# One-hot tiles of a gate matrix: tokens interleaved in pairs instead of in fours

## The chip, the cores and the metric

The kernel runs on one core of a Trainium2 chip. The metric is the device time of one execution in microseconds. Before the change it is 3146.83 us, the median of three runs (3141.98 to 3147.86).

## The reference

The reference is a decoder trunk of two layers over 512 tokens of width 1024. In each layer a mixer (differential attention, a short convolution and gated linear attention) is followed by PEER, a mixture of 16384 experts of one neuron each. Only PEER matters here. Each of its 8 heads scores 128 keys twice, takes the 16 best of each half, combines them and keeps the 16 best pairs; a pair names the expert `e1 * 128 + e2`, and a softmax over the 16 scores is its gate:

```python
e1 = jnp.take_along_axis(i1, ci // PEER_TOPK, axis=-1)
e2 = jnp.take_along_axis(i2, ci % PEER_TOPK, axis=-1)
experts = (e1 * PEER_NKEYS + e2).reshape(T, hk)
gates = jax.nn.softmax(sc, axis=-1).reshape(T, hk)
...
hb = jax.nn.gelu(jnp.einsum('tkd,td->tk', ub, xb), approximate=False)
return jnp.einsum('tk,tkd->td', gb * hb, vb)
```

So each token has 128 chosen experts (8 heads of 16), with rows `ub` and `vb` taken from two tables of 16384 rows.

## The kernel before

Of the 512 tokens, the last 128 are done by gathering rows (`gathered`, L719): GpSimd fetches one row per token at a time (L715), and VectorE multiplies and sums it (L723, L732). The first 384 tokens are done densely: for each chunk `c` of 128 experts, TensorE computes the hidden values of all 384 tokens (`hidden`, L639, tile `psh`, 24 matmuls of 384 columns), ScalarE applies the gelu (L645), and later, in a second sweep, the hidden values are multiplied by a gate (L813) and by the table `v` (`accumulate`, L824, tiles `pv`, matmuls of 512 columns). The gate is zero for every expert that a token didn't choose. f32 values are split into a high and a low part (`split`, L629: a cast on ScalarE at L630 and a subtraction on VectorE at L631), and each product takes three matmuls (`mm3`, L73 to L77).

The gates of all 384 tokens and 16384 experts are the gate matrix `G` in DRAM. It is built while the first sweep runs. `route` (L878) finds, for 128 tokens, the expert numbers and gates, and leaves them transposed as f16 tiles with 128 chosen experts in the partitions and the tokens along the free dimension: `E1` and `E2` (the two halves of the expert's number) and `GH` and `GL` (the gate, high and low). `gate_matrix` (L952) then takes 16 tokens at a time, which is one one-hot tile. VectorE writes four tiles of 128 partitions by 2048 f16:

- `A` (L964) is 1 where the row number equals the token's `E1`, `B` (L965) where it equals its `E2`; the row number comes from the constant `iota4`.
- `AH` (L966) and `AL` (L967) are `A` times the gate's high and low part.

For each token, TensorE then multiplies `B` by `AH` and by `AL` into one 128 by 128 block of `psg` (L972, L973), which is the token's gates for all experts. Four tokens fill one PSUM tile of 512 columns, which ScalarE evacuates (L975), and a DMA on ScalarE's queue writes the 16 tokens to `G` (L976). In the profile the tiles are called `oha` (A), `ohb` (B), `ohh` (AH) and `ohl` (AL). PSUM pool `psA`, from which `psg` comes, has four buffers, `B`, `AH` and `AL` have two each, `A` has one.

The tokens lie interleaved in these tiles: in the free dimension the order is group of four tokens, then row number 0 to 127, then the token in the group. So the VectorE operations read and write runs of four f16, and the 128 columns that TensorE reads for one token, as weights and as columns that it streams, are four f16 apart.

The order of the work is set by the program: the loop at L762 goes over the 72 chunks of the first sweep and 3 more, and after each chunk's `hidden` it draws from a generator as much routing and one-hot work as costs 2.72 us by an estimate written in the code (4.6 for one one-hot tile), and some steps of `gathered`. There are 24 one-hot tiles per layer, in three bursts of eight, and routing between them; 48 tiles in all, each with 32 pairs of weight load and matmul.

Of the kernel before, what the change touches and what calls it, by code (L numbers as in the profile page):

```python
# [10 lines left out]
F16 = mybir.dt.float16  # L11
# [8 lines left out]
P = 128  # L20
# [26 lines left out]
OHT = 16  # L47
# [12 lines left out]
def bc(ap, pattern):  # L60
    return bass.AP(tensor=ap.tensor, offset=ap.offset, ap=[ap.ap[0]] + pattern)


class K:
# [35 lines left out]
    def constants(self, scratch):  # L100
        nc, cp = self.nc, self.cp
        self.identb = cp.tile([P, P], BF16, name="identb")
        nc.scalar.copy(self.identb, self.ident)
        self.one = cp.tile([P, 1], F32, name="one")
        nc.vector.memset(self.one, 1.0)
        self.causal = cp.tile([P, P], BF16, name="causal")
        nc.gpsimd.memset(self.causal, 0.0)
        nc.gpsimd.affine_select(out=self.causal, in_=self.causal, compare_op=OP.is_ge, fill=-1.0e30,
                                base=0, pattern=[[-1, P]], channel_multiplier=1)
        self.starts = cp.tile([P, 16], F16, name="starts")  # L110
        self.dstart = cp.tile([P, 16], F16, name="dstart")
        self.iota16 = cp.tile([P, 16], F16, name="iota16")
        for j in range(16):
            nc.vector.memset(self.starts[:, j:j + 1], float(GRP_START[j]))
            nc.vector.memset(self.dstart[:, j:j + 1], float(GRP_START[j] - (GRP_START[j - 1] if j else 0)))
            nc.vector.memset(self.iota16[:, j:j + 1], float(j))
        self.iota4 = cp.tile([P, P, 4], F16, name="iota4")
        nc.gpsimd.iota(self.iota4, pattern=[[1, P], [0, 4]], base=0, channel_multiplier=0,
                       allow_small_or_imprecise_dtypes=True)
        used = 0  # L120

        def temp(*shape):
            nonlocal used
            n = math.prod(shape)
            t = scratch[:, used:used + n]
            used += n
            return t.rearrange("p (a b) -> p a b", b=shape[1]) if len(shape) > 1 else t

        pos_i = temp(TB).bitcast(I32)
        nc.sync.dma_start(pos_i, self.ins["positions"].rearrange("(b p) -> p b", p=P))  # L130
        pos = temp(TB)
        nc.vector.tensor_copy(pos, pos_i)
        ang = temp(TB, 8)
        for j in range(8):
            nc.vector.tensor_scalar(ang[:, :, j], pos, INV_FREQ[j], None, op0=OP.mult)
        res = []
        for name, shift in (("cos", 0.25), ("sin", 0.0)):
            n = temp(TB, 8)
            nc.vector.tensor_scalar(n, ang, 1.0 / (2 * math.pi), shift, op0=OP.mult, op1=OP.add)
            nc.vector.tensor_scalar(n, n, MAGIC, None, op0=OP.add)  # L140
            nc.vector.tensor_scalar(n, n, MAGIC, None, op0=OP.subtract)
            r = temp(TB, 8)
            prev = ang
            for c in TWO_PI:
                nc.vector.scalar_tensor_tensor(r, n, -c, prev, op0=OP.mult, op1=OP.add)
                prev = r
            if shift:
                nc.vector.tensor_scalar(r, r, math.pi / 2, None, op0=OP.add)
            nc.vector.tensor_scalar(r, r, 3.1415925, -3.1415925, op0=OP.min, op1=OP.max)
            t = cp.tile([P, TB, 8], F32, name=name)  # L150
            nc.scalar.activation(t, r, AF.Sin)
            res.append(t)
        self.cos, self.sin = res
# [43 lines left out]
        lo = self.act.tile([P, KD, T], F32R, tag="alo", name="alo")  # L197
        return hi, lo

    # ---------------------------------------------------------------- mixer  # L200
    def mixer(self, L):
        nc, tc, ins = self.nc, self.tc, self.ins
        lam_init = 0.8 - 0.6 * math.exp(-0.3 * L)
# [399 lines left out]
            self.head_out(of, ggain, mgh[:, :, t0:t0 + P], mgl[:, :, t0:t0 + P])  # L603
            yield 4

    # ---------------------------------------------------------------- peer
    def peer(self, L, xh, xl, rest):
        nc, tc, ins = self.nc, self.tc, self.ins
        G = self.dr.tile([NCH // GE, P, TD // TBAT, GE * TBAT], F32, tag="G", name="G")
# [342 lines left out]
    def gate_matrix(self, bt, E1, E2, GH, GL, G, hp):  # L952
        nc = self.nc
        stg = hp.tile([P, NCH, TBAT], F32, tag="stg", name="stg")
        for o in range(TBAT // OHT):
            t0 = bt * TBAT + o * OHT
            ng = OHT // 4
            tok = lambda t: bc(t[:, t0:t0 + OHT], [[4, ng], [0, P], [1, 4]])
            io = bc(self.iota4, [[0, ng], [4, P], [1, 4]])
            B = hp.tile([P, ng, P, 4], F16, tag="ohb", name="ohb")  # L960
            A = hp.tile([P, ng, P, 4], F16, tag="oha", name="oha", bufs=1)
            AH = hp.tile([P, ng, P, 4], F16, tag="ohh", name="ohh")
            AL = hp.tile([P, ng, P, 4], F16, tag="ohl", name="ohl")
            nc.vector.tensor_tensor(A, io, tok(E1), op=OP.is_equal)  # L964
            nc.vector.tensor_tensor(B, io, tok(E2), op=OP.is_equal)  # L965
            nc.vector.tensor_tensor(AH, A, tok(GH), op=OP.mult)  # L966
            nc.vector.tensor_tensor(AL, A, tok(GL), op=OP.mult)  # L967
            yield 4.6
            for g in range(ng):
                ps = self.psA.tile([P, 4, P], F32, tag="a", name="psg")  # L970
                for j in range(4):
                    nc.tensor.matmul(ps[:, j], B[:, g, :, j], AH[:, g, :, j], start=True, stop=False)  # L972
                    nc.tensor.matmul(ps[:, j], B[:, g, :, j], AL[:, g, :, j], start=False, stop=True)  # L973
                q = o * OHT + g * 4
                nc.scalar.activation(stg[:, :, q:q + 4].rearrange("p e t -> p t e"), ps, AF.Copy, scale=1.0 / GSCALE)  # L975
        nc.scalar.dma_start(G[:, :, bt].rearrange("g p w -> p g w"), stg.rearrange("p (g e) t -> p g (e t)", e=GE))  # L976
# [70 lines left out]
```

## Time and profile before

| | |
|---|---|
| Runs, median of three | 3146.83 us |
| Profiled execution, first to last instruction (its span) | 3145.6 us |
| Mean granted TensorE clock | 0.995 |
| One-hot matmuls (L972, L973), number | 768 + 768 |
| One-hot matmuls, mean duration of one | 297 and 298 ns |
| VectorE's four one-hot operations, number and mean of one | 4 × 48, 1.22 us |
| Evacuations of `psg` on ScalarE, number and mean of one | 192, 1.108 us |

The profiled execution has no time of its own beside its span; the span is 1.2 us under the median of the runs and inside their range, so sums against it are compared with the median. PE is TensorE's matmuls and PEld its weight loads, which overlap with them; DVE is VectorE, ACT ScalarE, POOL GpSimd. Matmuls are pipelined, so durations of neighbours overlap and what one costs is read from the distance of starts.

### The profile page before, as it was taken

The numbers are of one execution on the slowest core, as the hardware profiler recorded it, in microseconds if no ns is written. First come the engines' busy times: TensorE is split into PE (matmuls) and PEld (weight loads), VectorE is DVE, ScalarE is ACT, GpSimd is POOL, SyncE is SP. The second block draws the span as 40 slices with busy tenths as digits, with TensorE's granted clock in tenths as the row PEclk, the third lists the DMA queues.
The fourth block names the chain that finished last, engine by engine and source line by source line (L and its number), as shares of the span: only waits on it lengthen the run. The fifth ranks groups of instructions, "written<-read, shape, count | busy, mean of one in ns | idle before, by whom it ended". The sixth has DMA issues, their size and how long they took to land.

```text
span 3145.6 us, 45595 instructions
## 1 busy us (share of the span) xinstructions
PE 3083.6 (98%) x16742; PEld 2742.6 (87%) x16742; DVE 2473.3 (79%) x5079; ACT 1269.1 (40%) x1874; POOL 731.4 (23%) x543
## 2 busy tenths in 40 slices
PE   8999999999999999999999999999999999999998
PEld 7777889999999999788878788999999999987886
DVE  5776999968678787877766769998677878878777
ACT  5243345455333333333352533455553333323333
POOL 0000000211355554322200000002113555453221
PEclk9999999999999999999999999999999999999999
DMA  4112247788998888999722212478899988989996
GB/s 120 54 54 80 94 135 233 251 286 271 320 345 326 326 317 303 361 335 333 283 75 68 68 66 94 156 227 269 269 293 339 329 326 322 324 313 351 329 344 237
DMA packets 335665, 757.03 MB, mean 241 GB/s; under 512 B 30001, under 2 KB 192209, under 8 KB 331345
## 3 DMA queue, kind: packets, MB, share of 16 engines
q1 hardware_dynamic: 141904, 407.00, 36.5%
q0 software_dynamic: 73728, 268.47, 24.2%
q10 hardware_dynamic: 119808, 78.66, 8.0%
q8 instruction: 131, 2.15, 0.3%
q14 instruction: 94, 0.76, 0.1%
HBM read 673.28 MB, written 80.74 MB: 240 GB/s over the span
## 4 chain that ended last, share of the span: by engine, by line
PE 79%; DVE 6%; issue 6%; DMA 4%; POOL 3%; ACT 2%; SPq 0%; POOLq 0%; ACTq 0%; DVEq 0%
PE psh L77 9%; PE psh L75 9%; PE psh L76 9%; PE pv L77 9%; PE pv L76 9%; PE pv L75 9%; POOL row L715 3%; DMA row<-in_v_rows,idx 3%; PE psg L972 3%; PE psg L973 3%; PE psp L77 2%; PE psp L76 2%; PE psp L75 2%; PE psq L76 2%; PE psq L77 2%
## 5 line engine op out<-in xcount | busy, mean ns | idle before, releaser
L715 POOL DMA_INDIRECT row<-in_u_rows,idx x256 | 375.1, 1465 | 1407.5 <-DVE si L873 689.5
L75 PE MATMUL psh<-ahi,uh 128*128 128x384 f32 x2048 | 693.1, 338 | 2.0 <-ACT ht L645 2.0
L77 PE MATMUL psh<-ahi,ul 128*128 128x384 f32 x2048 | 688.4, 336 | 6.5 <-DVE ul L631 6.5
L76 PE MATMUL psh<-alo,uh 128*128 128x384 f32 x2048 | 687.3, 336 | 0.0
L75 PE MATMUL pv<-vh,wh 128*128 128x512 f32 x1536 | 597.6, 390 | 7.7 <-ACT wh L815 7.7
L77 PE MATMUL pv<-vh,wl 128*128 128x512 f32 x1536 | 601.3, 392 | 0.0
L76 PE MATMUL pv<-vl,wh 128*128 128x512 f32 x1536 | 600.6, 391 | 0.0
L715 POOL DMA_INDIRECT row<-in_v_rows,idx x256 | 339.1, 1324 | 595.2 <-DVE yacc L732 547.4
L631 DVE TENSOR_TENSOR ul<-uraw,uh 128x1024 fp32r<-128x1024 f32 x288 | 350.9, 1221 | 138.5 <-ACT uh L630 127.2
L630 ACT CAST uh<-uraw 128x1024 fp32r<-128x1024 f32 x288 | 302.5, 1052 | 315.4 <-PE psh L76 217.1
L645 ACT ACTIVATE ht<-psh 128x384 f32<-128x384 f32 x256 | 125.2, 489 | 709.0 <-PE psh L77 708.9
L75 PEld LDWEIGHTS psh<-ahi,uh 128*128 128x128 f32 x2048 | 387.4, 189 | 7.0 <-ACT ht L645 2.6
L77 PEld LDWEIGHTS psh<-ahi,ul 128*128 128x128 f32 x2048 | 386.3, 189 | 7.2 <-DVE ul L631 7.2
L76 PEld LDWEIGHTS psh<-alo,uh 128*128 128x128 f32 x2048 | 386.7, 189 | 4.1
L801 DVE TENSOR_TENSOR vl<-vraw,vh 128x1024 fp32r<-128x1024 f32 x256 | 312.7, 1221 | 79.4 <-issue 63.2
L75 PEld LDWEIGHTS pv<-vh,wh 128*128 128x128 f32 x1536 | 288.7, 188 | 67.1 <-ACT wh L815 10.0
L77 PEld LDWEIGHTS pv<-vh,wl 128*128 128x128 f32 x1536 | 289.2, 188 | 62.3 <-DVE wl L801 1.9
L76 PEld LDWEIGHTS pv<-vl,wh 128*128 128x128 f32 x1536 | 289.0, 188 | 59.5 <-DVE vl L801 1.0
L732 DVE SCALAR_TENSOR_TENSOR yacc<-row,wk,yacc 128x1024 f32<-128x1024 f32 x254 | 325.8, 1283 | 10.3 <-DMA row<-in_v_rows,idx 8.7
L723 DVE SCALAR_TENSOR_TENSOR gscr<-row,xg 128x1024 f32<-128x1024 f32 x256 | 312.5, 1221 | 13.9 <-DMA row<-in_u_rows,idx 12.0
L815 ACT CAST wh<-ht 128x384 fp32r<-128x384 f32 x256 | 130.8, 511 | 386.7 <-PE pv L76 218.9
L806 ACT CAST vh<-vraw 128x1024 fp32r<-128x1024 f32 x256 | 268.4, 1049 | 23.3 <-DMA vraw<-in_v_rows 22.1
(285 smaller groups left out, 4663.0 us busy)
## 6 DMA issues: line engine op xcount, KB each, us to landing
uraw<-in_peer_u SPq DMA_DIRECT2D x256, 512.0 KB, 4.8
vraw<-in_v_rows SPq DMA_DIRECT2D x256, 512.0 KB, 6.3
G<-stg ACTq DMA_DIRECT2D x48, 1024.0 KB, 6.5
g<-G SPq DMA_DIRECT2D x32, 1536.0 KB, 10.1
H<-ht ACTq DMA_DIRECT2D x144, 192.0 KB, 4.4
ht<-H SPq DMA_DIRECT2D x144, 192.0 KB, 5.7
wraw<-in_w_in SPq DMA_DIRECT2D x96, 256.0 KB, 2.9
uraw<-in_peer_w_q SPq DMA_DIRECT2D x32, 512.0 KB, 3.6
```

Of the source, the lines that this page charges most:

```text
L75: mm(ps, ah, bh, start=first, stop=False)
L76: mm(ps, ah, bl, start=False, stop=False)
L77: mm(ps, al, bh, start=False, stop=last)
L630: pin(nc.scalar.copy(hi, src))
L631: self.last = pin(nc.vector.tensor_tensor(lo, src, hi.bitcast(F32), op=OP.subtract))
L645: pin(nc.scalar.activation(hs[c], ps, AF.Gelu))
L715: nc.gpsimd.indirect_dma_start(out=r, out_offset=None, in_=ins[name], in_offset=bass.IndirectOffsetOnAxis(ap=idx[:, k:k + 1], axis=0))
L723: nc.vector.scalar_tensor_tensor(sc, r, 1.0, xg, op0=OP.mult, op1=OP.mult, accum_out=hd[:, k:k + 1])
L732: nc.vector.scalar_tensor_tensor(yacc, r, wk[:, k:k + 1], yacc, op0=OP.mult, op1=OP.add)
L801: self.last = pin(nc.vector.tensor_tensor(lo, src, hi.bitcast(F32), op=OP.subtract))
L806: pin(nc.scalar.copy(vh[c], vs[c]))
L815: pin(nc.scalar.copy(wh[c], hs[c]))
```

## The change

The tokens are interleaved in pairs: the order in the free dimension is pair of tokens, row number, token in the pair. The constant that holds the row numbers has two copies of each number instead of four. The VectorE operations have the same number of elements; their token operand now consists of runs of two f16, each read 128 times before the next. The four tokens of one PSUM tile now come from two pairs, and the 128 columns of a token are two f16 apart. The number and the order of the instructions on all engines, the buffers and the DMAs are the same.

```diff
-        self.iota4 = cp.tile([P, P, 4], F16, name="iota4")
-        nc.gpsimd.iota(self.iota4, pattern=[[1, P], [0, 4]], base=0, channel_multiplier=0,
+        self.iota2 = cp.tile([P, P, 2], F16, name="iota2")
+        nc.gpsimd.iota(self.iota2, pattern=[[1, P], [0, 2]], base=0, channel_multiplier=0,
...
-            ng = OHT // 4
-            tok = lambda t: bc(t[:, t0:t0 + OHT], [[4, ng], [0, P], [1, 4]])
-            io = bc(self.iota4, [[0, ng], [4, P], [1, 4]])
-            B = hp.tile([P, ng, P, 4], F16, tag="ohb", name="ohb")
-            A = hp.tile([P, ng, P, 4], F16, tag="oha", name="oha", bufs=1)
-            AH = hp.tile([P, ng, P, 4], F16, tag="ohh", name="ohh")
-            AL = hp.tile([P, ng, P, 4], F16, tag="ohl", name="ohl")
+            ng = OHT // 2
+            tok = lambda t: bc(t[:, t0:t0 + OHT], [[2, ng], [0, P], [1, 2]])
+            io = bc(self.iota2, [[0, ng], [2, P], [1, 2]])
+            B = hp.tile([P, ng, P, 2], F16, tag="ohb", name="ohb")
+            A = hp.tile([P, ng, P, 2], F16, tag="oha", name="oha", bufs=1)
+            AH = hp.tile([P, ng, P, 2], F16, tag="ohh", name="ohh")
+            AL = hp.tile([P, ng, P, 2], F16, tag="ohl", name="ohl")
...
-            for g in range(ng):
+            for g in range(OHT // 4):
                 ps = self.psA.tile([P, 4, P], F32, tag="a", name="psg")
                 for j in range(4):
-                    nc.tensor.matmul(ps[:, j], B[:, g, :, j], AH[:, g, :, j], start=True, stop=False)
-                    nc.tensor.matmul(ps[:, j], B[:, g, :, j], AL[:, g, :, j], start=False, stop=True)
+                    at = (slice(None), g * 2 + j // 2, slice(None), j % 2)
+                    nc.tensor.matmul(ps[:, j], B[at], AH[at], start=True, stop=False)
+                    nc.tensor.matmul(ps[:, j], B[at], AL[at], start=False, stop=True)
```

## The prediction

> **What bounds the kernel now.** I read the page first: its engine totals and the chain that ended last.
>
> ```profile
> span 3145.6 us, 45595 instructions
> PE 3083.6 (98%) x16742; PEld 2742.6 (87%) x16742; DVE 2473.3 (79%) x5079; ACT 1269.1 (40%) x1874; POOL 731.4 (23%) x543
> PE 79%; DVE 6%; issue 6%; DMA 4%; POOL 3%; ACT 2%; SPq 0%; POOLq 0%; ACTq 0%; DVEq 0%
> ```
>
> TensorE carries 79% of the chain. The next question is whether it is also the bound where the changed code runs. The second layer's gate stage is cut here into its three bursts of eight one-hot tiles (first, third and fifth row) and the routing between them. Columns: window, its length, busy time of PE, PEld, DVE, ACT and POOL, granted clock, DMA share, GB/s.
>
> ```profile
> 2013.00:2093.00 80.00, 80.00 (x541) 78.30 (x541) 71.89 (x175) 49.31 (x59) 3.78 (x4) 1.00 0.69 211
> 2093.00:2160.00 67.00, 67.00 (x392) 66.95 (x391) 61.73 (x162) 30.41 (x42) 9.44 (x8) 1.00 0.77 261
> 2160.00:2241.00 81.00, 81.00 (x551) 79.29 (x549) 67.35 (x75) 47.29 (x57) 15.50 (x11) 1.00 0.87 277
> 2241.00:2274.00 33.00, 33.00 (x194) 32.97 (x193) 17.57 (x20) 12.11 (x19) 4.68 (x5) 1.00 0.83 275
> 2274.00:2355.00 81.00, 81.00 (x550) 79.29 (x550) 61.86 (x66) 47.26 (x57) 14.80 (x12) 1.00 0.87 274
> sum 342.00, PE 342.00 PEld 336.79 DVE 280.40 ACT 186.37 POOL 48.20; mean PE 68.40 PEld 67.36 DVE 56.08 ACT 37.27 POOL 9.64
> ```
>
> TensorE never idles in these 342 us at full granted clock, so time taken off its stream comes off the kernel, until VectorE (133.6 of the first 147 us) or the DMA engines (0.87) stand in the way. A busy PE is not a PE at its peak, so the timeline of TensorE comes next, at the start of a burst: start, duration, instruction.
>
> ```profile
> 452.72 0.33 PE L76 MATMUL psh<-alo,uh 128*128 128x384 f32 x1
> ...
> 453.41 0.34 PE L77 MATMUL psh<-ahi,ul 128*128 128x384 f32 x1
> 453.59 0.29 PE L972 MATMUL psg<-ohh,ohb 128*128 128x128 f16 x1
> 453.69 0.30 PE L973 MATMUL psg<-ohl,ohb 128*128 128x128 f16 x1
> 453.81 0.30 PE L972 MATMUL psg<-ohh,ohb 128*128 128x128 f16 x1
> 453.93 0.30 PE L973 MATMUL psg<-ohl,ohb 128*128 128x128 f16 x1
> ...
> 456.42 0.30 PE L972 MATMUL psg<-ohh,ohb 128*128 128x128 f16 x1
> ```
>
> ```profile
> 1299.81 0.39 PE L75 MATMUL pv<-vh,wh 128*128 128x512 f32 x1
> ...
> 1301.40 0.39 PE L76 MATMUL pv<-vl,wh 128*128 128x512 f32 x1
> ```
>
> Durations overlap, so starts are what to read. The 384-column matmuls start 0.1725 us apart (452.72 to 453.41, four steps), the 512-column ones 0.227 us apart (seven steps): 128 more columns cost 0.0545 us, and 0.009 us is left for each load and matmul pair. The one-hot matmuls have only 128 columns, and should on that scale start 0.0635 us apart. They start 0.1187 us apart (453.69 to 456.42, 23 steps). Taking 0.009 off, a column costs 0.86 ns where the others pay 0.43: a factor of two. What differs is the operand: before the change the columns of one token lie four f16, 8 bytes, apart; the fast matmuls read 4-byte columns that touch.
>
> **The change part by part.** No instruction is added, removed or moved; only the iota constant halves (outside the loops, once). What changes is the address pattern of three reads: TensorE's columns (8 bytes apart, now 4), its weights likewise, and the token operand of four VectorE operations (runs of four, now two).
>
> TensorE's columns. Four-byte spacing is what the f32 rows above read at 0.43 ns a column, so I take 0.0635 us for a pair. The lower bound is the only 16-bit matmul with touching columns, whose successor starts 0.06 us later:
>
> ```profile
> 191.60 0.22 PE L439 MATMUL pss<-causal,identb 128*128 128x128 bf16 x1
> 191.66 0.33 PE L438 MATMUL pss<-kT,qz 128*128 128x128 f32 x1
> ```
>
> The upper bound is no gain, 0.1187. By the middle one, each pair saves 0.0552 us; 48 tiles of 32 pairs make 1536 pairs, so 84.8 us for the kernel, 42.4 per layer, 1.77 per tile. With 0.06 it would be 90 us. [...]
>
> TensorE's weights. These are the groups by form; columns: count | busy us, mean ns | idle before.
>
> ```profile
> L973 PEld LDWEIGHTS <-ohb 128*128 128x128 f16 x768 | 90.2, 117 | 1.4
> L439 PEld LDWEIGHTS <-identb 128*128 128x128 bf16 x64 | 6.3, 99 | 4.7 <-issue 2.4
> L75 PEld LDWEIGHTS psh<-ahi,uh 128*128 128x128 f32 x2048 | 387.4, 189 | 7.0 <-ACT ht L645 2.6
> ```
>
> A load lasts 117 ns against 99 with touching columns; it should come down between. It runs beside the previous matmul, so I cost it at nothing. Its cover gets thinner, though: in the one-hot stream each load starts with a matmul and the next matmul starts when it ends. If that end were a hard condition, the cover is gone at 99 ns; the f32 loads speak against it, since they last 189 ns in a stream that starts every 173. That is the third rival.
>
> VectorE. Four operations a tile, 192 in all:
>
> ```profile
> L965 DVE TENSOR_TENSOR ohb<-iota,E 128x2048 f16<-128x2048 f16 x48 | 58.7, 1222 | 29.9 <-PE psg L973 29.9
> L966 DVE TENSOR_TENSOR ohh<-oha,GH 128x2048 f16<-128x2048 f16 x48 | 58.6, 1220 | 4.1 <-PE psg L972 4.1
> L923 DVE TENSOR_TENSOR ge<-ci,starts 128x2048 f16<-128x2048 f16 x8 | 18.3, 2282 | 0.0
> L920 DVE TENSOR_TENSOR pr<-pr 128x2048 f16<-128x2048 f16 x8 | 9.8, 1219 | 0.1
> L920 DVE TENSOR_TENSOR pr<-pr 128x1024 f16<-128x1024 f16 x16 | 11.2, 699 | 0.1
> L920 DVE TENSOR_TENSOR pr<-pr 128x256 f16<-128x256 f16 x8 | 3.5, 442 | 0.1
> L469 DVE TENSOR_TENSOR ho<-po,ry 128x512 f32<-128x512 f32 x8 | 5.5, 692 | 0.4
> ```
>
> They take 1.22 us for 2048 elements, two a cycle; L923, whose token operand repeats single elements, takes 2.28, one a cycle. Runs of two are not in the trace as a repeated operand. Bounds: 1.22 (as now) and 2.28 (single elements); a gain is excluded, because the unbroken 2048-element row (L920) is no shorter. The nearest row for runs of two is L920's last pass, 256 elements in 442 ns. From 2048 and 1024 elements (1219, 699) an element costs 0.508 ns, so 256 would take 309 at two a cycle and 439 at one. It runs at one. But there every run of two is followed by a jump of 32 bytes in all three operands, while in the change the output and the iota are unbroken and the token operand reads one 4-byte word again and again, which L469 does with an f32 word at full pace: 512 elements at one a cycle in 692 ns, as many cycles as 1024 packed ones in 699. I take 1.22 us, as nearer to the last, and keep 2.28 as the rival. [...]
>
> What is late next. In the first burst and the routing behind it (2013 to 2160), TensorE's 147 us would shrink by eight tiles' 14.2 to 132.8, below VectorE's own 133.6. VectorE's look-ahead is two one-hot buffers and three weight chunks, so some waits stay, an estimated 4 us: about 138 us, and 5 of 14.2 us are not collected. In the other 195 us TensorE would need 166.7; VectorE 146.8, ScalarE 106.7. The DMA engines were busy for 0.87×81 + 0.83×33 + 0.87×81 = 168 us there, so they would be full. What they moved in each fortieth of the span:
>
> ```profile
> GB/s 120 54 54 80 94 135 233 251 286 271 320 345 326 326 317 303 361 335 333 283 75 68 68 66 94 156 227 269 269 293 339 329 326 322 324 313 351 329 344 237
> ```
>
> They are not yet at their most: 276 GB/s would become 323, and later slices hold up to 361. I charge 3 us.
>
> ScalarE's four evacuations per tile are not hidden within a burst:
>
> ```profile
> L975 ACT ACTIVATE stg<-psg 128x512 f32<-128x512 f32 x192 | 185.0, 1108 | 7.0 <-PE psg L973 7.0
> L630 ACT CAST uh<-uraw 128x1024 fp32r<-128x1024 f32 x288 | 302.5, 1052 | 315.4 <-PE psh L76 217.1
> L645 ACT ACTIVATE ht<-psh 128x384 f32<-128x384 f32 x256 | 125.2, 489 | 709.0 <-PE psh L77 708.9
> ```
>
> 4 × 1.108 = 4.43 us against 32 × 0.0635 = 2.03 on TensorE. But four PSUM buffers take a whole tile, and the next tile comes at least 24 × 0.1725 = 4.14 us later; a cycle of one tile and one chunk needs 5.97 us of ScalarE against 6.17 of TensorE. So nothing is charged, with the tightest margin of all.
>
> Sum: 42.4 − 5 − 3 = 34.4 per layer, about 69 us in both. The profiled span is 3145.6 us, 1.2 below the median of 3146.83 and inside the runs' 3141.98 to 3147.86. So 3146.8 − 69 = 3078 us.
>
> **The rivals.** *VectorE falls to one element a cycle.* Each of 192 operations costs 1.06 us more, 4.25 per tile. VectorE then needs 133.6 + 34 = 167.6 us where there are 147, 118.9 where there are 114, and 61.9 + seven tiles' 29.8 = 91.7 where there are 81: 36 us more per layer, and some 6 of waits. That is 84 us more, 3231, whatever TensorE gains. In the first stretch it takes over from (147 − 133.6 − 4)/32 = 0.3 us more per operation; with about 0.55 more the stage as a whole is slower than today (137.6 + 150.8 + 96 × 0.56 = 342). For: the L920 row. Against: no jumps here.
>
> *TensorE's reading is not what is slow.* Then the factor of two has another cause, such as any spacing other than touching, and two f16 apart is as slow as four. Time: 3147. For: no row shows 16-bit columns with gaps smaller than four. Against: the f32 rows read the same byte spacing at full pace. [...]
>
> *The weight load binds.* If a matmul must wait for the whole load, a pair takes 0.100 us (99 ns and the start), so 0.0187 × 1536 = 29 us gross; VectorE and the DMA engines cover that nearly whole: 3120 us.
>
> **How the numbers follow.** Forecast 0.60, VectorE slow 0.19, no change 0.15, load-bound 0.06. The likeliest case gives 3078; its own range is 3052 (0.06 a pair, nothing lost: 90, and a few us of run-to-run spread) to 3100 (9 us of the first stretch and, if the DMA engines hold up the later bursts, half of their 28.3: 23 per layer). The load-bound and unchanged cases lie up to 3153; together these hold about 0.8, so the range is 3052 to 3153 and leaves out the slow VectorE. A measurement of this kernel can tell about 0.2%, 6 us, from no change. Faster: 0.60 + 0.06 = 0.66; same 0.15; slower 0.19.
>
> **What would show it.** Right: one-hot matmuls starting about 0.064 us apart; the four VectorE groups still at 1.22 us; a burst of a tile 2.0 instead of 3.8 us; TensorE's first idle time in the gate stage, before psh, released by VectorE's ul. Wrong: VectorE groups at 2.28 us with TensorE waiting for ohh or ul; starts still 0.119 apart; starts at 0.100 with each load ending at a matmul's start; or a DMA share near 1.0 with VectorE waiting for row.

## The result, and the profile after

The changed kernel takes 3074.93 us (median of four runs, 3068.26 to 3076.22), the kernel before 3145.01 us beside it (3141.98 to 3147.86). The ratio is 0.9774, 95% interval 0.9763 to 0.9786: 70 us faster. The forecast was 3078 us. The time of every kernel is the median of its fast executions; of the kernel with columns in pairs one execution of four was slow, at 4738.76 us, and isn't counted.

First the page of the changed kernel: the span, the busy time of each engine, and the chain that ended last.

```profile
span 3066.5 us, 45595 instructions
PE 2996.6 (98%) x16742; PEld 2657.9 (87%) x16742; DVE 2470.3 (81%) x5079; ACT 1268.5 (41%) x1874; POOL 739.7 (24%) x543
PE 74%; issue 7%; DVE 7%; POOL 4%; DMA 3%; ACT 3%; ACTq 1%; SPq 0%; POOLq 0%; DVEq 0%
```

PE has 87 us less busy time, PEld 85 less, and no other engine has changed by more than 9. TensorE's part of the chain fell from 79% to 74%, and ScalarE's DMA issues (ACTq) have come in with 1%. The profiled execution took 3068.26 us (its span is 1.8 us less), 6.7 us under the median of the runs, so the account of the whole gain at the end of this text uses a later profile of the same kernel, whose time is the median.

Now the one-hot burst itself. This is TensorE's timeline in the changed kernel, from the last matmul before a tile to the first one behind it: start, duration, instruction.

```profile
459.60 0.34 PE L77 MATMUL psh<-ahi,ul 128*128 128x384 f32 x1
459.78 0.23 PE L973 MATMUL psg<-ohh,ohb 128*128 128x128 f16 x1
459.85 0.22 PE L974 MATMUL psg<-ohl,ohb 128*128 128x128 f16 x1
...
461.57 0.22 PE L974 MATMUL psg<-ohl,ohb 128*128 128x128 f16 x1
461.60 0.42 PE L75 MATMUL psh<-ahi,uh 128*128 128x384 f32 x1
```

The tile lasts 1.82 us (459.78 to 461.60), and from 459.85 to 461.57 are 30 steps of 0.0573 us. Before, a step was 0.1187 us and a tile took 3.70 us. The groups by form show the same, and also what did not change (count | busy us, mean ns | idle before):

```profile
L973 PE MATMUL psg<-ohh,ohb 128*128 128x128 f16 x768 | 93.9, 219 | 0.4 <-ACT stg L976 0.4
L974 PEld LDWEIGHTS <-ohb 128*128 128x128 f16 x768 | 74.5, 97 | 0.7 <-issue 0.7
L964 DVE TENSOR_TENSOR oha<-iota,E 128x2048 f16<-128x2048 f16 x48 | 58.5, 1218 | 0.1
L966 DVE TENSOR_TENSOR ohh<-oha,GH 128x2048 f16<-128x2048 f16 x48 | 58.5, 1218 | 0.0
L976 ACT ACTIVATE stg<-psg 128x512 f32<-128x512 f32 x192 | 186.0, 1121 | 12.2 <-issue 9.9 <-PE psg L974 2.3
```

A matmul's record is 78 ns shorter (219 against 297), a load's 20 ns (97 against 117). VectorE's operations take 1.22 us as before. The four evacuations of a tile still take 4.5 us beside a burst of 1.82 us, and TensorE waited 0.4 us for them in the whole run.

For the stage as a whole, here is the second layer cut at the ends of the bursts: the first burst with the routing behind it, the second with its routing, and the third. The first fence is before, the second after. Columns: window, its length, busy time of PE, PEld, DVE, ACT and POOL, granted clock, DMA share, GB/s.

```profile
2013.50:2160.80 147.30, 147.30 (x933) 145.53 (x933) 133.92 (x337) 79.74 (x101) 13.22 (x11) 1.00 0.73 234
2160.80:2274.70 113.90, 113.90 (x741) 112.16 (x741) 84.82 (x95) 59.37 (x75) 20.37 (x17) 1.00 0.86 275
2274.70:2354.90 80.20, 80.20 (x545) 78.65 (x545) 61.16 (x64) 47.16 (x57) 14.58 (x11) 1.00 0.88 276
```

```profile
1972.20:2108.70 136.50, 134.12 (x932) 132.53 (x931) 133.15 (x337) 79.54 (x100) 13.28 (x11) 0.99 0.78 252
2108.70:2208.20 99.50, 99.23 (x742) 97.78 (x740) 84.39 (x95) 59.25 (x75) 23.38 (x17) 1.00 0.93 315
2208.20:2273.50 65.30, 65.30 (x546) 64.20 (x545) 57.47 (x60) 44.33 (x53) 16.71 (x10) 1.00 0.95 312
```

By the median of the 48 tiles, a tile takes 1.888 us less (3.705 before, 1.817 after), and eight of them make 15.1 us for each stretch. The second and third collect 14.4 and 14.9 of it, and in them TensorE is still busy throughout, at a DMA share of 0.93 and 0.95. The first collects 10.8, and there VectorE is busy for 133.15 of 136.5 us (2.2 us of its idle time wait for ScalarE's cast, 1.1 for TensorE) while TensorE idles 2.4. The first layer reads 10.2, 14.6 and 14.9. So the gate stages give 79.8 us together.

Not all of that arrives. From the end of the first layer's last burst to the second layer's first one-hot matmul it took 1218.5 us before and 1221.0 after, and from the second layer's last burst to the end 790.7 and 793.0: 4.8 us are given back. The rest of the difference between the two spans, 4.1 us, lies before the first one-hot matmul (453.6 against 449.5 us), where the change does nothing; that start differs from run to run, and in the repetition below it is at 452.8.

### The profile page after: what moved, and what is told of

Same layout as the page of the kernel before. It is cut to its first block, busy times and chain, and to the rows that moved or that the text cites. A ratio compares the mean times of both kernels' runs of the same rounds, so it can differ in the third digit from the quotient of the medians.

```text
span 3066.5 us, 45595 instructions
## 1 busy us (share of the span) xinstructions
PE 2996.6 (98%) x16742; PEld 2657.9 (87%) x16742; DVE 2470.3 (81%) x5079; ACT 1268.5 (41%) x1874; POOL 739.7 (24%) x543
## 4 chain that ended last, share of the span: by engine, by line
PE 74%; issue 7%; DVE 7%; POOL 4%; DMA 3%; ACT 3%; ACTq 1%; SPq 0%; POOLq 0%; DVEq 0%
PE pv L77 9%; PE pv L75 9%; PE pv L76 9%; PE psh L75 8%; PE psh L77 8%; PE psh L76 8%; POOL row L715 4%; PE psp L77 2%; PE psp L76 2%; PE psp L75 2%; DMA row<-in_v_rows,idx 2%; PE psq L76 2%; PE psq L77 2%; PE psq L75 2%; PE pst L545 1%
## 5 line engine op out<-in xcount | busy, mean ns | idle before, releaser
L715 POOL DMA_INDIRECT row<-in_u_rows,idx x256 | 390.6, 1526 | 1315.9 <-DVE si L873 669.5
L715 POOL DMA_INDIRECT row<-in_v_rows,idx x256 | 331.5, 1295 | 601.5 <-DVE yacc L732 565.7
L645 ACT ACTIVATE ht<-psh 128x384 f32<-128x384 f32 x256 | 125.3, 489 | 612.4 <-PE psh L77 605.5
```

The lines of the kernel that those rows point to most:

```text
L645: pin(nc.scalar.activation(hs[c], ps, AF.Gelu))
L715: nc.gpsimd.indirect_dma_start(out=r, out_offset=None, in_=ins[name], in_offset=bass.IndirectOffsetOnAxis(ap=idx[:, k:k + 1], axis=0))
```

## Where the rest of the gain went: two waits to explain

Before the change TensorE waits for nothing in the gate stages. In the changed kernel one long wait comes in each first stretch, and others follow at the end of the stages. The waits are given here from one start to the next; the idle time that the profile prints in brackets is some 0.3 us less. The long one is 3.2 us in the first layer and 2.7 in the second. TensorE's timeline in the first:

```profile
527.22 0.34 PE L77 MATMUL psh<-ahi,ul 128*128 128x384 f32 x1
530.40 0.45 PE L75 MATMUL psh<-ahi,uh 128*128 128x384 f32 x1 [2.85 <-ACT ht L645]
...
531.16 0.52 PE L75 MATMUL psh<-ahi,uh 128*128 128x384 f32 x1
531.48 0.52 PE L76 MATMUL psh<-alo,uh 128*128 128x384 f32 x1
```

Behind the wait, matmuls of 384 columns start 0.32 us apart for about ten matmuls, where they start every 0.173 us otherwise. TensorE waited for ScalarE's gelu (L645), because no buffer of `psh` was free. ScalarE's timeline says why the gelu was late; ACTq is a DMA issue.

```profile
518.31 0.38 ACTq L977 DMA_DIRECT2D G<-stg  x1
...
519.79 7.12 ACTq L769 DMA_DIRECT2D H<-ht  x1
526.94 1.28 ACT L898 ACT_TABLE_LOAD   x1 [6.24 <-issue]
528.23 0.31 ACT L898 ACTIVATE gt<-gt 128x128 f32<-128x128 f32 x1
528.56 1.28 ACT L645 ACT_TABLE_LOAD   x1
529.86 0.49 ACT L645 ACTIVATE ht<-psh 128x384 f32<-128x384 f32 x1
```

The issue of a small write (192 KB) of hidden values, behind the 1 MB write of 16 tokens to `G` on the same queue, held ScalarE for 7.12 us; then came the routing's exponential with a load of its table, and only then the gelu, with a load of its own. VectorE had finished the exponential's input (L897) at 523.6 us, so in this kernel it was the issue that held ScalarE here. The other waits are at the end of the stage: one of 2.3 us at 763.6 in the first layer, behind such an issue of 8.14 us, and waits of 1.4 and 1.0 us in the second. The source view of those issues, before and after (duration min/median/max in ns, first and last start):

```profile
L769 ACTq DMA_DIRECT2D H<-ht x144: 326/326/5220, 414.7 to 2369.0; - x144
```

```profile
L769 ACTq DMA_DIRECT2D H<-ht x144: 326/326/8141, 411.9 to 2289.2; - x144
```

In all, the 144 issues held ScalarE for 72 us before and for 168 after: with shorter bursts the writes to `G` come closer together. The slower kernel with eights below fits this: its 144 issues take 47 us and none lasts over 0.341. TensorE's waits for that gelu in the whole run, before and after (total us, times, longest):

```profile
PE psh L75 <- ACT ht L645: 2.0, 2, 1.0
```

```profile
PE psh L75 <- ACT ht L645: 10.3, 6, 2.8
```

So there were two questions for the experiments: whether the streamed columns, and they alone, are what became faster, and whether the missing microseconds belong to VectorE, which the prediction blamed, or to ScalarE's queue, which the waits name.

## The experiments on the columns

**Weights in pairs, columns in fours.** Only `B` takes the new order.

```diff
+            IA, IB = 4, 2
...
+            B = hp.tile([P, OHT // IB, P, IB], F16, tag="ohb", name="ohb")
+            A = hp.tile([P, OHT // IA, P, IA], F16, tag="oha", name="oha", bufs=1)
...
+                    col = (slice(None), n // IA, slice(None), n % IA)
+                    wgt = (slice(None), n // IB, slice(None), n % IB)
+                    nc.tensor.matmul(ps[:, j], B[wgt], AH[col], start=True, stop=False)
```

> Only the weights (tile ohb) lie two f16 apart; the columns that TensorE streams (ohh, ohl) stay four f16, 8 bytes, apart as before the change. Theory 'columns': what the change sped up is the stream of columns, so nothing is gained here: one-hot matmuls start 0.118 us apart, weight loads come down to about 97 ns in the record or stay at the distance of starts, time 3145 us (within 6). Rival 'weights': the load, which before the change ended exactly where the next matmul started, was what held the stream: starts 0.057 us apart, time 3075 us. If both reads share one limit, starts lie between, at 0.085 to 0.10 us, and the time at 3100 to 3125 us.

Measured: 3142.30 us, ratio 0.9994 (0.9984 to 1.0003). A stretch of twelve steps on TensorE's timeline:

```profile
451.76 0.30 PE L978 MATMUL psg<-ohh,ohb 128*128 128x128 f16 x1
...
453.16 0.30 PE L978 MATMUL psg<-ohh,ohb 128*128 128x128 f16 x1
```

That is 0.117 us a pair, as in the kernel before. The order of the weights is worth at most 0.002 us a pair, 3 us in the whole kernel, which the times can't tell from nothing.

**Columns in pairs, weights in fours.** The same kernel with the two numbers exchanged.

```diff
+            IA, IB = 2, 4
```

> The other half: the streamed columns (ohh, ohl) lie two f16 apart, the weights (ohb) stay four f16 apart. Theory 'columns': the whole gain is here, starts 0.057 to 0.065 us apart with loads still some 115 ns in the record, time 3075 us (within 6). Rival 'weights': starts stay at 0.118 us, time 3145 us. If both reads share one limit: 0.085 to 0.10 us, 3100 to 3125 us.

Measured: 3069.32 us, ratio 0.9762 (0.9742 to 0.9781): the whole of the gain. The loads by form, and fifteen steps of the timeline:

```profile
L979 PEld LDWEIGHTS <-ohb 128*128 128x128 f16 x768 | 87.8, 114 | 0.0
```

```profile
451.83 0.22 PE L978 MATMUL psg<-ohh,ohb 128*128 128x128 f16 x1
...
452.72 0.22 PE L979 MATMUL psg<-ohl,ohb 128*128 128x128 f16 x1
```

The loads still last 114 ns, and the pairs start 0.059 us apart. A matmul therefore doesn't wait for the end of its load's record, and the rival in which the load binds is refuted.

**Eights.** All tiles in groups of eight, so that the columns are 16 bytes apart. My theory for the kernel before was that TensorE reads up to eight touching bytes per column step, so that 16 bytes apart would be as slow as 8.

```diff
+            IA, IB = 8, 8
```

> All four one-hot tiles hold the tokens in eights, so columns and weights lie eight f16, 16 bytes, apart; VectorE reads runs of eight and stays at 1.22 us. Theory 'eight bytes a cycle': TensorE reads up to 8 touching bytes per column step, and any column in another 8 bytes costs one full step, so 16 bytes are as slow as 8: starts 0.118 us, time 3145 us (within 6). [...]

Measured: 3396.73 us, ratio 1.0806 (1.0788 to 1.0824). My theory fell: it said 0.118 us a step, and a step takes 0.233. The end of a burst and the matmuls behind it:

```profile
467.36 0.41 PE L976 MATMUL psg<-ohl,ohb 128*128 128x128 f16 x1
...
474.36 0.41 PE L976 MATMUL psg<-ohl,ohb 128*128 128x128 f16 x1
...
474.89 0.52 PE L76 MATMUL psh<-alo,uh 128*128 128x384 f32 x1
475.21 0.52 PE L77 MATMUL psh<-ahi,ul 128*128 128x384 f32 x1
...
477.27 0.33 PE L75 MATMUL psh<-ahi,uh 128*128 128x384 f32 x1
477.44 0.33 PE L76 MATMUL psh<-alo,uh 128*128 128x384 f32 x1
```

Thirty steps take 7.00 us, 0.233 us each. With spacings of 4, 8 and 16 bytes, 128 columns take 0.057, 0.117 and 0.233 us: in proportion to the bytes that they span, 1.8 ns for every 16 bytes. The f32 rows of before fit the same number: 512 touching columns in 0.227 us are 1.77 ns for 16 bytes. Spacings above 16 bytes were not tried.

The gate stage grew by 122 us a layer, and only 24 × 32 × (0.2333 − 0.1187) = 88 us of that are the bursts. The rest lies behind them: the next matmuls start 0.32 us apart for about 2 us. The windows show the granted clock down where the bursts are, and at 0.50 already in the second half of this one (the last three columns: clock, DMA share, GB/s).

```profile
450.00:560.00 110.00, 110.00 (x504) 90.05 (x503) 69.51 (x162) 49.66 (x55) 2.04 (x2) 0.78 0.48 145
470.20:474.60 4.40, 4.40 (x21) 2.81 (x20) 0.00 (x0) 2.18 (x3) 0.00 (x0) 0.50 0.46 155
560.00:640.00 80.00, 80.00 (x442) 76.19 (x441) 67.50 (x178) 35.33 (x48) 12.46 (x10) 0.96 0.70 232
```

**Singles.** An interleave of one: the columns of a token touch, and VectorE's token operand repeats single elements.

```diff
+            IA, IB = 1, 1
```

> No interleaving: a token's 128 columns touch. VectorE's token operand then repeats single elements and runs at one element a cycle: 2.28 us instead of 1.22 for each of the four operations. This is the price of the rival on VectorE, made on purpose, with TensorE at its best: starts 0.056 to 0.057 us. By the sum on record (36 us more per layer and 6 of waits) 3231 us; if waits behind VectorE cost TensorE more (idle times long enough to lower the granted clock), 3240 to 3280 us. If VectorE's look-ahead hides the extra work, 3075 to 3100 us.

Measured: 3225.82 us, ratio 1.0260 (1.0243 to 1.0277). VectorE's group, and where TensorE waits for it:

```profile
L964 DVE TENSOR_TENSOR oha<-iota,E 128x2048 f16<-128x2048 f16 x48 | 109.4, 2280 | 0.0
```

```profile
PE psg L976 <- DVE ohl L967: 43.8, 32, 1.8
```

TensorE's pairs start 0.055 to 0.056 us apart, hardly faster than in pairs: with touching f16 a column takes 0.43 to 0.44 ns. VectorE's operations take 2.28 us, like L923's in the prediction, and VectorE is busy for 375.9 of the first stage's 380.3 us. The granted clock was 0.98, 0.93 and 0.91 there (440 to 600, to 720, to 820 us). This is the prediction's first rival with its price: it said 36 us more per layer plus waits and 3231 us; the stage is 39 us longer and the kernel takes 3226. Of the interleaves tried (one, two, four, eight), two is the smallest that keeps VectorE at 1.22 us and the largest at which TensorE is near its fastest (0.057 us a pair; singles 0.055 to 0.056).

## The experiments on what was not collected

**The changed kernel again**, in the company of the next three.

> The changed kernel as it is, as the point of comparison for the three other kernels of this call: 3075 us (within 5), with TensorE idle for about 3 us behind the first burst of each layer and some ten matmuls at a lower granted clock after that.

Measured: 3075.05 us, ratio 0.9780 (0.9767 to 0.9793). The first stretches last 136.8 us in both layers and the long wait comes back with 3.2 and 3.0 us, so neither is chance.

**A smaller step.** The code's own budget for routing and one-hot work behind each chunk goes from 2.72 to 2.55 us, which spreads VectorE's work of the first stretch over more chunks.

```diff
-DVE_STEP = 2.72
+DVE_STEP = 2.55
```

> The changed kernel with the estimate of VectorE work drawn per chunk lowered from 2.72 to 2.55 us, so that routing and one-hot tiles spread over more chunks. Theory: the 9 us that the first bursts do not give back (4.9 in the first layer, 4.5 in the second) are VectorE's lateness, which makes ScalarE wait at the gates' exponential, and so TensorE; with less per chunk it goes away: 3066 us. Rival 'order': the wait stays as long as the exponential stands ahead of the gelu in ScalarE's queue: 3072 to 3077 us. Rival 'fuller queues': ScalarE or the DMA engines are what hold TensorE there, and the spread helps them only a little: 3070 to 3075 us.

Measured: 3082.37 us, ratio 0.9807 (0.9793 to 0.9820), and so 7 us slower than the changed kernel. The expectation was missed: a wait of 2.2 us stays in the first stretch, now for VectorE's `ul`, and the stage ends so late that the second sweep stands still at its start: VectorE's multiplication by the gates (L813) waits twice, 15.5 us together, for what is read back from `G`, and TensorE waits for the products. In the first layer:

```profile
PE pv L75 <- ACT wh L815: 9.9, 1, 9.9
```

**The exponential later.** In the routing, the budget's step is taken ahead of the gates' exponential instead of behind it, so that the exponential should fall where ScalarE isn't held.

```diff
         gt = ...
+        yield 2.0
         nc.scalar.activation(gt, gt, AF.Exp)
...
-        yield 2.0
```

> The changed kernel with the generator's step of 2.0 us moved from behind the routing's small operations to between the subtraction on VectorE and the exponential on ScalarE, so that the exponential is issued later than its input, behind more of the chunks' work. Theory 'VectorE late': the wait at the exponential gets shorter or goes: 3066 to 3070 us if it is issued at least one chunk later, 3075 us if it falls into the same chunk. Rival 'fuller queues': 3075 us.

Measured: 3073.87 us, ratio 0.9769 (0.9755 to 0.9782), no different from the changed kernel. The wait moved and stayed: 4.1 us in the first layer for the gelu, 1.0 for the gelu and 1.1 and 1.2 for `ul` in the second, with first stretches of 138.9 and 136.0 us.

**No exponential.** It leaves out the exponential of the gates, and with it the loads of its table.

```diff
-        nc.scalar.activation(gt, gt, AF.Exp)
```

> The changed kernel without the exponential of the gates (the softmax is left out of its numerator, so the gates are other numbers), which is the only operation of the routing on which ScalarE waits for VectorE at that place. Theory: TensorE's idle time of 3 us behind each first burst comes from ScalarE waiting at the head of its queue, so it goes: 3064 to 3067 us, some of it from the table loads of the activation that fall away. Rival 'VectorE itself binds': TensorE waits for the low halves of the weights (ul) at the same place instead, for as long: 3072 to 3077 us.

Measured: 3066.77 us, ratio 0.9755 (0.9742 to 0.9769), about 8 us less than the changed kernel. The long wait is gone, but the first stretch only fell to 135.7 us in both layers, and VectorE is busy for 135.1 of it in the first. Of TensorE's waits there are now nine for VectorE's low parts (seven of them in the first stretches), where there were two:

```profile
PE psh L77 <- DVE ul L631: 10.4, 9, 3.5
```

So most of the loss of the first stretch doesn't hang on this wait of ScalarE's. Which part of the 8 us comes from the exponentials themselves and which from other places with a table load stays open.

**The gate writes on SyncE's queue**, and then, instead, **the hidden writes on SyncE's queue.** Each separates the two writes that share ScalarE's queue.

```diff
-        nc.scalar.dma_start(G[:, :, bt]...
+        nc.sync.dma_start(G[:, :, bt]...
```

> The changed kernel with the write of the gate matrix (G) issued from SyncE's queue instead of ScalarE's; the write of the hidden values (H) stays on ScalarE's. In the changed kernel, issuing H occupies ScalarE's queue for 168 us in all, against 72 before the change, up to 8 us at a time right behind a G. Theory 'queue behind G': this is what makes the exponential and the gelu late and costs TensorE some 9 us behind the first bursts and some 5 at the end of the stages: the issues of H fall to 0.33 us each, and the time to 3061 us (3058 to 3066). Rival 'DMA engines full': the writes are as slow on any queue, and the loads of the weights on SyncE's queue now wait behind G: TensorE waits for ul, 3075 us or more. Rival 'VectorE late': the H issues get short, but TensorE's gap behind the first bursts stays: 3070 to 3075 us.

```diff
-                nc.scalar.dma_start(H[c], hs.pop(c))
+                nc.sync.dma_start(H[c], hs.pop(c))
```

> The changed kernel with the write of the hidden values (H) issued from SyncE's queue, where it stands between the loads of the weights, and the write of G still on ScalarE's. Theory 'queue behind G': ScalarE is free of the waits, so the gaps on TensorE go as well; but an H that waits for its gelu holds the loads behind it, which are three ahead: 3061 to 3068 us. Rival 'DMA engines full': 3075 us or more. Rival 'VectorE late': 3070 to 3075 us.

Measured: 3192.82 us, ratio 1.0155 (1.0141 to 1.0169), and 3126.69 us, ratio 0.9940 (0.9927 to 0.9954). Both are far slower than the changed kernel and miss the theory's times, for a reason that the expectations had named without pricing it so high: SyncE's queue issues the loads of the tables, and these now stand behind the writes, which wait for their data. ScalarE's casts wait for the loaded rows, 9.3 us in two waits in the changed kernel and far longer here; with the gate writes there and with the hidden writes there:

```profile
ACT uh L630 <- DMA uraw<-in_peer_u: 295.8, 60, 9.0
```

```profile
ACT uh L630 <- DMA uraw<-in_peer_u: 212.6, 76, 9.1
```

What can still be read: with the gate writes moved no hidden write holds ScalarE for over 0.356 us, so the write ahead of it on the same queue is what held it. And with the hidden writes moved the first stretch lasts 138.0 and 137.5 us although the long wait is gone.

**The same two on GpSimd's queue**, which has room in this stage (GpSimd is busy for 13.28 of the 136.5 us of the changed kernel's first stretch).

```diff
-                nc.scalar.dma_start(H[c], hs.pop(c))
+                nc.gpsimd.dma_start(H[c], hs.pop(c))
```

> The changed kernel with the write of the hidden values (H) issued from GpSimd's queue, so that it stands behind neither G nor the loads of the weights; GpSimd's row gathers share the queue with it. Theory 'DMA engines full, VectorE late' as the runs before left it: TensorE's long gap behind the first bursts goes, but VectorE's lateness stays there as short waits for ul, so the first stretch is still 136 to 138 us; the gap at the end of the stage gets shorter: 3068 to 3073 us. Rival 'queue behind G' after all: first stretch 133 to 135 us, 3061 to 3066 us. If the gathers behind a waiting H come late, VectorE waits for row: 3080 us or more.

```diff
-        nc.scalar.dma_start(G[:, :, bt]...
+        nc.gpsimd.dma_start(G[:, :, bt]...
```

> The changed kernel with the write of the gate matrix (G) issued from GpSimd's queue. Theory 'DMA engines full, VectorE late': ScalarE is no longer held, first stretch 136 to 138 us all the same, 3068 to 3073 us if GpSimd prepares the 2048 short pieces of a G fast enough; the gathers stand behind G, and if they come late VectorE waits for row, and one-hot tiles wait for free stg buffers: 3080 to 3150 us. Rival 'queue behind G': 3061 to 3066 us.

Measured, hidden writes moved: 3067.80 us, ratio 0.9757 (0.9743 to 0.9770). The long wait for the gelu is replaced by three waits for `ul` of 1.1 to 1.8 us, and the first stretch still lasts 136.4 us in both layers. Waits of 3.2 and 1.0 us at the end of the stage stay (in a profiled execution that took 4.8 us more than the median), but no longer for the gelu.

```profile
PE psh L77 <- DVE ul L631: 12.7, 8, 3.3
```

At the end of the first layer's stage TensorE now waits for `wh`, and ScalarE 4.1 us for rows of `v`. Their loads stand on SyncE's queue behind the read of `G`, which waits for the last write of `G` (us in total, times, longest):

```profile
SPq L791 <- DMA G<-stg: 10.3, 1, 10.3
```

That wait is 4.9 us in the kernel before and 10.2 in the changed kernel.

Measured, gate writes moved: 3064.78 us, ratio 0.9749 (0.9735 to 0.9762), the lowest median of all. The changed kernel wasn't repeated beside it; by the ratios it is 8 to 10 us faster. The hidden writes' issues, SyncE's wait for the last write of `G` in the first layer, and the first stretch of the second layer:

```profile
L769 ACTq DMA_DIRECT2D H<-ht x144: 326/326/345, 415.7 to 2286.9; - x144
```

```profile
SPq L791 <- DMA G<-stg: 2.6, 1, 2.6
```

```profile
1971.60:2108.50 136.90, 134.11 (x933) 132.52 (x931) 133.87 (x337) 79.00 (x100) 22.97 (x19) 0.99 0.77 251
```

No issue lasts over 0.345 us. GpSimd's busy time in the stretch rose from 13.28 to 22.97 us with eight instructions more, by an estimate 1.2 us for each write of `G`. The waits at the end of the stage are gone: 1217.3 us lie between the layers' gate stages and 790.9 behind the second, within 1.2 us of what they were before the change. Against the repetition, 4.4 and 2.1 us are gained behind the stages and 3.4 in them. So the time falls into the rival's range and the first stretch into the theory's: it is as long as ever, 136.9 us, with VectorE busy for 133.9 of it. TensorE's long wait for the gelu is there too, 3.1 us in both layers, although no issue holds ScalarE. Now ScalarE waits for VectorE's input of the exponential:

```profile
527.64 0.31 ACT L898 ACTIVATE gt<-gt 128x128 f32<-128x128 f32 x1 [4.56 <-DVE gt L897]
```

So both readings were right, each for its own place. In the first stretch it is VectorE's lateness: 135.7 to 138.9 us in every variant except the smaller step (140.2, with other work drawn per chunk) and the gate writes on SyncE's queue (153.6 and 148.7), whichever engine the wait is written against. This is read from VectorE's busy time; no run took work from VectorE and left the rest as it was. At the end of the stage it is the writes of `G` on ScalarE's queue, in two ways: the hidden write behind them holds ScalarE, and the last of them lands late, which delays the loads behind its read. Moving the hidden writes takes away only the first; moving the gate writes takes away both.

## Why the prediction was right, point by point

**The columns.** Right in mechanism, and a little low in size: 0.0635 us a pair was forecast and 0.0573 measured, less even than the 0.06 that was taken as the lower bound. The 0.009 us that the f32 rows left over for each pair, and that I added, isn't paid by these pairs: 0.0573 us is 128 times 0.448 ns. The gain before losses is 24 × 1.888 = 45.3 us a layer instead of 42.4. The factor of two between fours and pairs was the right thing to look at, and its reason is the spacing of the streamed columns, as the two halves of the change show.

**The weights.** Costed at nothing, and worth next to nothing by the run with the weights alone (0.117 us a pair). The load fell to 97 ns, just under the 99 that I gave as its floor.

**VectorE.** 1.22 us was taken against 2.28, and 1.218 measured. Two and one elements a cycle are the prediction's names for the rates of these two times for 2048 elements; the length of a cycle is in no trace. The row with runs of two that speaks for the slower rate (256 elements in 442 ns) was put down to its jumps of 32 bytes. The changed kernel, which has no such jumps, loses nothing, which fits; no run tests the jumps themselves. Singles take 2.28 us.

**What is late next.** The first stretch was forecast at about 138 us with 5 us of its gain lost; it is 136.5 to 137.0 with 4.3 to 4.9 lost. The later bursts were charged 3 us a layer for the DMA engines, and lost 0.6 to 0.9: at 312 to 315 GB/s, close to the 323 that the prediction worked out, neither TensorE nor VectorE waited for a transfer; in each layer ScalarE's cast waited once for a loaded chunk, 4.8 and 4.5 us, which it hadn't before. ScalarE was charged nothing "with the tightest margin of all", and this is the term that was mis-sized. The margin of evacuations against PSUM buffers held (0.4 us of waits). What the prediction didn't count is the issue of DMAs on ScalarE's queue: a step that is not moved still comes closer to its neighbours when the work between them shrinks. With the late landing of the last write of `G`, it costs some 2.5 us a layer behind the stage.

**The sum.** Forecast 42.4 − 5 − 3 = 34.4 a layer. By the trace of the changed kernel's repetition, whose time is the median: the two stages give 37.5 and 39.6, 3.2 and 2.3 are lost behind them, and the start of the first differs by 0.8, together about 72.3 us of span, against 70 us between the medians. The errors (2.9 too little for the columns, about 2 too much for the DMA engines, 2.5 to 3 missing for ScalarE's queue) partly cancel, and that the forecast came within 3 us owes something to this luck. The upper end of the likeliest case, 3100 us, doesn't follow from its own terms: 23 us is what would be lost in a layer, which leaves 19 and gives 3108.

**The sign to look for.** TensorE's first idle time in the gate stage was to be released by VectorE's `ul`. It was released by ScalarE's `ht`. The detail was wrong. The cause behind it, VectorE's lateness, was the one named, as the runs without the exponential and with the hidden writes on GpSimd's queue show: take ScalarE's delay away, and waits for `ul` stand in its place.

**The rivals.** That TensorE's reading is not what is slow fell with the first experiment pair. For the columns that TensorE streams, spacings of 4, 8 and 16 bytes take 0.057, 0.117 and 0.233 us.

## What to carry to other kernels

Read the distance of starts per column, and compare it with the fastest stream in the same trace: in this kernel a matmul of 128 columns that lie apart pays for the bytes that they span, for the streamed operand (0.057, 0.117 and 0.233 us at 4, 8 and 16 bytes) and hardly for the weights (0.002 us at most between 4 and 8). An interleave has two sides (TensorE's pairs take 0.057 us in twos and 0.1187 in fours, VectorE's operations 1.22 us in twos and 2.28 in singles), so look for the value at which neither pays. And when a stage becomes shorter, look at the DMA issues on the queues of computing engines: a small write behind a large one can hold the engine (here up to 8.14 us), and the wait then shows up under another name. Look also at what waits for the large write to land (here the read of `G`, 10.2 us).

## What the runs showed of the hardware that I had not expected

- TensorE's time for 128 f16 columns is proportional to their spacing from 4 to 16 bytes (57, 117, 233 ns), about 1.8 ns for each 16 bytes spanned; columns that touch, 2 bytes apart, take 55 to 56 ns. The spacing of the weights changed a pair by 0.002 us at most, though the load's record went from 97 to 114 ns.
- The granted clock can fall while the records show TensorE busy without a break: in the kernel with eights it is 0.50 from 470.2 to 474.6 us, in the second half of a burst of 7.3 us, and the f32 matmuls behind the burst start 0.32 us apart until 476.8 instead of 0.173. In the changed kernel the same pace follows idle times of 2.85, 2.38 and 1.98 us (granted clock 0.50 from 531 to 534 us and from 766.6 to 769). What lowers the clock in the burst was not shown.
- A DMA issue with a median of 0.326 us held ScalarE for up to 8.14 us when a 1 MB write had been issued on the same queue 1.45 us before. With the large writes on GpSimd's queue the longest was 0.345 us, and on SyncE's 0.356.
